# A two-block trunk on one core: wider operations in the state space setup and scan, another order of v's tiles, five tiles of u ahead

## The chip, the cores and the metric

The kernel runs on one core of a Trainium2 chip. The metric is the time of one execution on the device in microseconds (us). A core has five instruction queues that run in order, each its own: PE (matmul), DVE (vector), ACT (activation), POOL (a second, slower vector engine, which also issues gathers) and SP (which issues DMAs). PE's weight loads are listed as PEld. They meet only at semaphores. The activations, weights and tables lie in DRAM and are brought in by DMA.

## The reference

512 tokens of width 1024 pass two blocks, each a mixer and then an expert feed-forward ("peer"). Everything is float32. The second block's mixer has the state space layer that the change touches, and both blocks have the same feed-forward:

```
# state space (s5): 32 groups of 64 complex states, 16 channels each
x[t] = abar * x[t-1] + bbar @ u[t]          # abar, bbar from a, b and dt
y[t] = Re(C @ x[t]) + d * u[t]

# feed-forward (peer): 16384 experts, 8 heads, top 16 of each
scores -> top 16 pairs of keys per head -> eidx, gate
act = gelu(u[eidx] . h)                     # dot products with rows of u
out = sum(gate * act * v[eidx])             # rows of v
```

The output is the normalised sum of the residual stream after both blocks.

## The kernel before, in words

The program is written out in full, in Python, for all five queues; there is no scheduler. What sets the order is one object, `Env` (L29). Each gemm calls `E.tick()` after every 12 matmuls (L191 to 197). A tick runs functions that were deferred for it (`E.defer(n, fn)`), one step of each chain in `E.chains`, and `E.rate` steps of a filler, `E.fill`, a generator that issues a few instructions for any queue at each `yield`. `weave` (L79) makes one filler of several, each with a rate of its own. So work beside the gemms is spread over them by tick counts, and what a filler has left at the end is issued at once by `E.drain()` (L73).

Every float32 product is three matmuls, with both sides split in a high and a low part (`split`, L108: the high part by ACT at L111, the low one by DVE or POOL at L114; `mm3`, L117).

The stages, in time: the first mixer to about 625 us; the first feed-forward to 1946, whose steady stage with v begins near 1105; the second mixer to 2285; the second feed-forward, its steady stage from about 2768 to 3612.

*The setup of the state space layer* (`s5_setup`, L531) depends on weights alone. It is a filler beside the end of the first mixer: its gate gemm, `ret_out`, the merge gate and the last product (`add_gated`), then `E.flush()` and `E.drain()` at L1000 and 1001. It shares the filler with `mods`, which streams a second set of modulation weights (tile `ada`). POOL computes powers of the transition (the prelude); then come four quarters of eight groups. A quarter transposes its C on PE (L671), forms BB (L677 to 679), Q (nine powers, L688 to 690) and R (eight, L696 to 698) on POOL, multiplies Q by BB on PE (L708) and transposes R on PE (L722).

*The scan* (`Mix2.scan`, L1494) runs over 64 chunk states X on DVE, one column after the other, as a chain of the second mixer: three columns a tick. Beside it the gated recurrence of the same mixer (`scale`, `level`, `chain`, L1632 to 1700) goes between PE (ch, L1657), POOL (L1645, L1648) and DVE (tqd, L1643; tP, L1649).

*The feed-forward's steady stage* (`Peer.steady`) goes over the 128 blocks of 128 experts. The first L0 = 60 blocks had their product with u in the stage before, and their activations were put away (tile `old`); the other 68 ("new") are multiplied with u here: `s_step` loads a tile of u three ahead, splits the next and issues 24 matmuls (tile p) and a gelu (tile act). Each block then needs a tile of v: `v_load` (tile vr), `v_prep` (splits v to vh and vl, multiplies the activation by the gate G, splits that to wh and wl) and `v_mm` (18 matmuls, tile pv). The numbers at the head of `Peer` set how the two go together: LEAD tiles of u before the first v, S_END the step by which all of u is done. The fourth group of 128 tokens is done without matmuls, by POOL's gathers of rows of u and v (tile gr) and DVE's dot products and sums (L2296, L2301); SPARSE_END and VF set by which step of v these are through.

Of the kernel before, what the change touches and what calls it, by code (L numbers as in the profile page):

```python
# [526 lines left out]
TS = 8  # L527
# [3 lines left out]
def s5_setup(E, A, pool, ps):  # L531
# [133 lines left out]
    for q in range(4):  # L665
# [9 lines left out]
        tb_ = t("q1", [128, N, H], bufs=2)  # L675
# [7 lines left out]

        Q = t("Q", [128, N, TS + 1, H])
        R = t("R", [128, N, TS, H])
        for n in range(TS + 1):
            q1 = t("q1", [128, N, H], bufs=2)
            g_.tensor_tensor(Q[:, :, n, :], CT[:, 0], bc(f[:, n, 0, :]), op=ALU.mult)  # L688
            g_.tensor_tensor(q1, CT[:, 1], bc(f[:, n, 1, :]), op=ALU.mult)
            g_.tensor_tensor(Q[:, :, n, :], Q[:, :, n, :], q1, op=ALU.add)  # L690
            if n % 4 == 3:
                yield
        for n in range(TS):
            r1 = t("q1", [128, N, H], bufs=2)
            Rj = R[:, :, n, :]
            g_.tensor_tensor(Rj, BB[:, 0], bc(pw[:, n, 0, :]), op=ALU.mult)  # L696
            g_.tensor_tensor(r1, BB[:, 1], bc(f[:, n, 2, :]), op=ALU.mult)
            g_.tensor_tensor(Rj, Rj, r1, op=ALU.add)
            if n % 4 == 3:
                yield  # L700
        yield
        E.rate = E.S5_RATE
        nc.sync.dma_start(E.s5M[2, :, gs].rearrange("p g (n h) -> p g n h", h=H), Q[:, :, 1:, :])

        for g4 in range(0, N, 4):
# [92 lines left out]
class Mix1:  # L798
# [6 lines left out]
    def run(self):  # L805
# [98 lines left out]
        with tc.tile_pool(name="m1v", bufs=1) as vp:  # L904
            with tc.tile_pool(name="m1p", bufs=1, side="right") as pp:
                self.phi = pp.tile([128, 4, 512], F32R, name="phi")
                self.plo = pp.tile([128, 4, 512], F32R, name="plo")
                with tc.tile_pool(name="m1pt", bufs=1, side="right") as pt_:
                    self.pooling(pt_, pms)
                    self.keys(vp, chi, clo)  # L910
                with tc.tile_pool(name="m1f", bufs=1) as fp:
                    E.fill, E.rate = mod_filler(E, A, fp, psum, [("", m) for m in (2, 3, 4, 5)], 2, 2), 2.2
                    self.context_keys(m1, fp)
                    self.values(chi, clo)
                    for c in range(4):
                        W = ws.get()
                        for j in range(2):
                            pm = ps.tile([128, 512], F32, name="mm")
                            gemm_T(E, pm, W, self.phi, self.plo, j)
                            nc.scalar.activation(poolT[:, 2 * c + j, :], pm, AF.Copy)  # L920
                            E.tick()
                    while E.fill is not None:
                        E.tick()
                    E.flush()
                    self.context()
            with tc.tile_pool(name="m1k", bufs=1, side="right") as kp:
                self.decays(kp)
                E.flush()
# [21 lines left out]
        gp = tc.alloc_tile_pool(name="m1g", bufs=1)  # L950
        sp = tc.alloc_tile_pool(name="m1s", bufs=1)
        mods = mod_filler(E, A, Halves(E), psum, [("_2", m) for m in range(4)], 3, 2)
        E.fill, E.rate = weave((s5_setup(E, A, sp, ps), 0.6), (mods, 2.3)), 1.0
        ws.lo = ("dve",)
        rhi = gp.tile([128, 8, 512], F32R, name="rhi")
        rlo = gp.tile([128, 8, 512], F32R, name="rlo")
# [375 lines left out]
class Mix2:  # L1332
# [93 lines left out]
    def states(self):  # L1426
# [3 lines left out]
        self.X = X = self.xp.tile([128, NC5 + 1, 2, 32], F32, name="s5X")  # L1430
        Uc = up.tile([64, 32, TS, 16], F32, name="s5Uc")
        nc.gpsimd.memset(X[:, 0], 0.0)
        P1s = []
        for g8 in range(4):
            P1 = up.tile([128, 8, 128], F32, name="s5P", bufs=2)
# [50 lines left out]
    def unit_nat(self, c):  # L1486
        W = self.ws.get()
        for tb in range(4):
# [2 lines left out]
            self.nc.scalar.activation(self.vi[:, tb, 256 * c:256 * (c + 1)], pm, AF.Copy)  # L1491
            self.E.tick()

    def scan(self):  # L1494
        E, v, X = self.E, self.v, self.X
        a = self.gp.tile([128, 2, 32], F32, name="s5ra")
        b = self.gp.tile([128, 2, 32], F32, name="s5rb")
        for c in range(1, NC5):
            v.tensor_tensor(a, X[:, c], E.s5AR, op=ALU.mult)
            for i in range(2):  # L1500
                v.tensor_tensor(b[:, i, :], X[:, c, 1 - i, :], E.s5AI[:, i, :], op=ALU.mult)
            v.tensor_tensor(a, a, X[:, c + 1], op=ALU.add)
            v.tensor_tensor(X[:, c + 1], a, b, op=ALU.add)
            if c % 3 == 0:
                yield


    def s5_chunks(self):
# [217 lines left out]
class Peer:  # L1726
# [5 lines left out]
    LAG = 4  # L1732
    NQ, NT = 42, 8
    L0 = 60
    LEAD = 2
    S_END = 112
    RATE, RATE_T = 1.3, 1.3
    QT = 2
    WLO = "dve"
    SPARSE_END = 122  # L1740
    VF = 0.5

    def __init__(self, E, pfx, wq, key_rows, u, uT, v, AB, done, fill):
        self.E, self.pfx = E, pfx
# [494 lines left out]
    def v_prep(self, e, vp, spare=False):  # L2239
# [190 lines left out]
```

## Time and profile before

| | |
|---|---|
| runs | 3637.18, 3644.05, 3645.54 us; median 3644.05 |
| profiled execution | 3638.08 us, span 3636.3, granted clock 0.973 |
| PE busy | 3406.6 us, 94% of the span |
| DVE, ACT, POOL busy | 2829.1, 1380.6, 1117.7 us (78, 38, 31%) |
| moved from and to HBM | 744.52 MB read, 82.33 MB written |

Busy time is the time in which an engine has an instruction under way, and idle time is told with what ended it (the releaser). PE's share is an average: in the steady stages it is close to full, in the mixers it is not. The granted clock is PE's, 1 being 2.4 GHz. A single row's duration, on an engine that can be held up in the middle of an instruction, contains that delay.

### The profile page before, as it was taken

The page shows a single profiled execution, that of the slowest core. Times are in us where ns is not written, and L with a number is a line of the kernel's source. Part 1 is how long each engine was busy: PE and PEld are TensorE (multiplying, and loading weights), DVE is VectorE, ACT ScalarE, POOL GpSimd, SP SyncE. Part 2 cuts the span into 40 slices and gives each one's busy share as a digit, 9 for nine tenths or more (in the row PEclk, how much of TensorE's full clock was granted, in tenths as well). Part 3 has the DMA queues.
Part 4 walks back from the last instruction along what each step waited for, and adds up shares of the span by engine and source line. Part 5 has one row for each costly group of instructions (what it writes and reads, how often), then busy time and mean ns, then how long its engine had stood idle before and what let it go on. Part 6 is the DMA issues. An engine that isn't in the chain of part 4 may idle for free. (4 is left out here: it accounts for less than half of the span.)

```text
span 3636.3 us, 50853 instructions
## 1 busy us (share of the span) xinstructions
PE 3406.6 (94%) x18339; PEld 2992.4 (82%) x18339; DVE 2829.1 (78%) x6079; ACT 1380.6 (38%) x1930; POOL 1117.7 (31%) x1076
## 2 busy tenths in 40 slices
PE   8989887999998999999998888999998999999998
PEld 5878676999887888888886778899887888888886
DVE  6654743898996888888877685788996888888886
ACT  4223333332673333333334324432574333333333
POOL 3212675000003444444431432000001445444451
PEclk9999998999999999999998989999999999999999
DMA  5442754443459999999993213244457999999995
GB/s 189 137 148 71 217 172 104 131 135 126 176 201 327 359 345 352 339 338 348 329 322 115 70 57 103 95 141 139 143 206 269 341 373 325 350 341 336 348 323 193
DMA packets 418747, 830.20 MB, mean 228 GB/s; under 512 B 37948, under 2 KB 249776, under 8 KB 415424
## 3 DMA queue, kind: packets, MB, share of 16 engines
q1 hardware_dynamic: 344320, 558.41, 45.3%
q0 software_dynamic: 74176, 268.55, 20.3%
q8 instruction: 144, 2.36, 0.3%
q14 instruction: 107, 0.88, 0.1%
HBM read 744.52 MB, written 82.33 MB: 227 GB/s over the span
## 5 line engine op out<-in xcount | busy, mean ns | idle before, releaser
L2280 POOL DMA_INDIRECT gr<-in_peer_u_dram,rb x256 | 367.9, 1437 | 1406.5 <-DMA ur<-in_peer_u_tiles_dram 491.1
L118 PE MATMUL pv<-vh,wh 128*128 128x512 f32 x1512 | 602.3, 398 | 48.6 <-ACT wh L111 48.1
L120 PE MATMUL pv<-vh,wl 128*128 128x512 f32 x1512 | 604.3, 400 | 0.0
L119 PE MATMUL pv<-vl,wh 128*128 128x512 f32 x1512 | 594.6, 393 | 0.0
L2280 POOL DMA_INDIRECT gr<-in_peer_v_dram,rb x256 | 371.6, 1452 | 405.3 <-DVE accs L2301 343.0
L114 DVE TENSOR_TENSOR ul<-ur,uh 128x1024 fp32r<-128x1024 f32 x260 | 318.0, 1223 | 128.2 <-ACT uh L111 126.5
L118 PEld LDWEIGHTS pv<-vh,wh 128*128 128x128 f32 x1512 | 286.5, 189 | 126.7 <-ACT wh L111 75.2
L114 DVE TENSOR_TENSOR vl<-vr,vh 128x1024 fp32r<-128x1024 f32 x252 | 308.1, 1223 | 79.2 <-ACT vh L111 77.3
L118 PE MATMUL p<-hi,uh 128*128 128x384 f32 x1088 | 365.6, 336 | 1.4 <-ACT act L2074 1.4
L120 PE MATMUL p<-hi,ul 128*128 128x384 f32 x1088 | 365.7, 336 | 0.3 <-DVE ul L114 0.3
L119 PE MATMUL p<-lo,uh 128*128 128x384 f32 x1088 | 365.3, 336 | 0.0
L120 PEld LDWEIGHTS pv<-vh,wl 128*128 128x128 f32 x1512 | 286.1, 189 | 86.8 <-DVE wl L114 29.3
L118 PE MATMUL mm<-hi,uh 128*128 128x384 f32 x960 | 333.9, 348 | 3.6 <-ACT qT L1832 3.6
L119 PEld LDWEIGHTS pv<-vl,wh 128*128 128x128 f32 x1512 | 286.9, 190 | 52.6
L2301 DVE SCALAR_TENSOR_TENSOR accs<-gr,rb,accs 128x1024 f32<-128x1024 f32 x254 | 325.7, 1282 | 5.5 <-DMA gr<-in_peer_v_dram,rb 0.7
L120 PE MATMUL mm<-hi,ul 128*128 128x384 f32 x960 | 324.2, 338 | 4.5 <-DVE ul L114 4.5
L119 PE MATMUL mm<-lo,uh 128*128 128x384 f32 x960 | 323.0, 337 | 0.0
L2296 DVE SCALAR_TENSOR_TENSOR gr<-gr,hs 128x1024 f32<-128x1024 f32 x256 | 303.2, 1219 | 0.0
L111 ACT ACTIVATE vh<-vr 128x1024 fp32r<-128x1024 f32 x252 | 265.9, 1055 | 60.1 <-PE pv L120 30.8
L111 ACT ACTIVATE uh<-ur 128x1024 fp32r<-128x1024 f32 x260 | 272.6, 1048 | 5.5 <-DMA ur<-in_peer_u_tiles_dram 5.5
L118 PE MATMUL mm<-hi,whi 128*128 128x512 f32 (+1 forms) x656 | 262.3, 400 | 1.1 <-ACT hi L311 1.1
L120 PE MATMUL mm<-hi,wlo 128*128 128x512 f32 (+1 forms) x656 | 252.7, 385 | 1.3 <-DVE wlo L114 1.3
(625 smaller groups left out, 7079.5 us busy)
## 6 DMA issues: line engine op xcount, KB each, us to landing
ur<-in_peer_u_tiles_dram SPq DMA_DIRECT2D x256, 512.0 KB
vr<-in_peer_v_dram SPq DMA_DIRECT2D x252, 512.0 KB
raw<-in_w_in_dram SPq DMA_DIRECT2D x60, 512.0 KB
ada<-in_ada_w_dram SPq DMA_DIRECT2D x96, 256.0 KB
fG<-gst SPq DMA_DIRECT2D x12, 2048.0 KB
f_2G<-gst SPq DMA_DIRECT2D x12, 2048.0 KB
x<-in_ada_w_dram SPq DMA_DIRECT2D x64, 256.0 KB
raw<-in_peer_wq_dram SPq DMA_DIRECT2D x32, 512.0 KB
```

The source lines that it names most:

```text
L111: nc.scalar.activation(hi, src, AF.Copy)
L114: (nc.vector if e_lo == "dve" else nc.gpsimd).tensor_tensor(lo, src, hi.bitcast(F32), op=ALU.subtract)
L118: nc.tensor.matmul(out, a_hi, b_hi, start=start, stop=False)
L119: nc.tensor.matmul(out, a_hi, b_lo, start=False, stop=False)
L120: nc.tensor.matmul(out, a_lo, b_hi, start=False, stop=stop)
L2280: nc.gpsimd.indirect_dma_start(out=r, out_offset=None, in_=self.u if n < 128 else self.v, in_offset=bass.IndirectOffsetOnAxis(ap=self.eidx ...
L2296: nc.vector.scalar_tensor_tensor(r, r, 1.0, self.hs, op0=ALU.mult, op1=ALU.mult, accum_out=dots[:, j:j + 1])
L2301: nc.vector.scalar_tensor_tensor(accs, r, w[:, j:j + 1], accs, op0=ALU.mult, op1=ALU.add)
```

## The change

Five edits. (1) In the setup, Q is made in two parts of five and four powers, three POOL operations each, and R in two parts of four, three operations each on DVE; the setup's own rate in the weave goes from 0.6 to 1.0 a tick, and the line that raised the rate after a first quarter is gone. (2) The first mixer's earlier stream of modulation weights gets lag 3 for 2 and rate 2.3 for 2.2. (3) The scan goes over eight blocks of eight columns at once: seven steps inside the blocks, then seven from block to block with powers 1 to 8 of the transition, which the new `powers` computes. (4) In `Peer`, LEAD is 5 instead of 2 (the rule that orders the blocks keeps the 2, as WAIT), SPARSE_END 118 instead of 122 and VF 0.6 instead of 0.5. (5) `v_prep` issues the product with the gate first, and both of ACT's splits ahead of DVE's two.

```diff
@@ s5_setup
-        for n in range(TS + 1):
-            q1 = t("q1", [128, N, H], bufs=2)
-            g_.tensor_tensor(Q[:, :, n, :], CT[:, 0], bc(f[:, n, 0, :]), op=ALU.mult)
-            g_.tensor_tensor(q1, CT[:, 1], bc(f[:, n, 1, :]), op=ALU.mult)
-            g_.tensor_tensor(Q[:, :, n, :], Q[:, :, n, :], q1, op=ALU.add)
-            if n % 4 == 3:
-                yield
-        for n in range(TS):
...
-        yield
-        E.rate = E.S5_RATE
+        def combine(e, o, X, c0, c1, part):
+            k = part.stop - part.start
+            sh = [128, N, k, H]
+            x = [X[:, i, :, None, :].to_broadcast(sh) for i in range(2)]
+            c = [z[:, part, gs].rearrange("p n g -> p g n")[:, :, :, None].to_broadcast(sh) for z in (c0, c1)]
+            z = t("q2", [128, N, 5, H])[:, :, :k, :]
+            e.tensor_tensor(o[:, :, part, :], x[0], c[0], op=ALU.mult)
+            e.tensor_tensor(z, x[1], c[1], op=ALU.mult)
+            e.tensor_tensor(o[:, :, part, :], o[:, :, part, :], z, op=ALU.add)
+
+        for part in (slice(0, 5), slice(5, TS + 1)):
+            combine(g_, Q, CT, f[:, :, 0, :], f[:, :, 1, :], part)
+            yield
+        for part in (slice(0, 4), slice(4, TS)):
+            combine(v, R, BB, pw[:, :, 0, :], f[:, :, 2, :], part)
+            yield
+        yield
@@ Mix1.run
-                    E.fill, E.rate = mod_filler(E, A, fp, psum, [("", m) for m in (2, 3, 4, 5)], 2, 2), 2.2
+                    E.fill, E.rate = mod_filler(E, A, fp, psum, [("", m) for m in (2, 3, 4, 5)], 2, 3), 2.3
...
-        E.fill, E.rate = weave((s5_setup(E, A, sp, ps), 0.6), (mods, 2.3)), 1.0
+        E.fill, E.rate = weave((s5_setup(E, A, sp, ps), 1.0), (mods, 2.3)), 1.0
@@ Mix2
+        E.defer(2, self.powers)
...
     def scan(self):
-        for c in range(1, NC5):
-            v.tensor_tensor(a, X[:, c], E.s5AR, op=ALU.mult)
             for i in range(2):
-                v.tensor_tensor(b[:, i, :], X[:, c, 1 - i, :], E.s5AI[:, i, :], op=ALU.mult)
-            v.tensor_tensor(a, a, X[:, c + 1], op=ALU.add)
-            v.tensor_tensor(X[:, c + 1], a, b, op=ALU.add)
-            if c % 3 == 0:
-                yield
+        def add(to, frm, cR, cI):
+            v.tensor_tensor(a, frm.to_broadcast(sh), cR[:, :, None, :].to_broadcast(sh), op=ALU.mult)
             for i in range(2):
+                v.tensor_tensor(b[:, :, i], frm[:, :, 1 - i].to_broadcast(half), cI.to_broadcast(half), op=ALU.mult)
+            v.tensor_tensor(a, a, to, op=ALU.add)
+            for i in range(2):
+                v.tensor_tensor(to[:, :, i], a[:, :, i], b[:, :, i], op=ALU.subtract if i else ALU.add)
+
+        for j in range(1, 8):
+            add(Xb[:, :, j], Xb[:, :, j - 1], self.pR[:, 0:1], self.pI[:, 0:1])
+            yield
+        for k in range(1, 8):
+            add(Xb[:, k], Xb[:, k - 1, 7:8], self.pR, self.pI)
+            yield
@@ Peer
-    LEAD = 2
+    LEAD = 5
+    WAIT = 2
-    SPARSE_END = 122
-    VF = 0.5
+    SPARSE_END = 118
+    VF = 0.6
...
-            have = self.s_by[i - 1 - self.LEAD] if i > self.LEAD else 0
+            have = self.s_by[i - 1 - self.WAIT] if i > self.WAIT else 0
@@ Peer.v_prep
-        split(nc, raw, vh, vl, "act", "dve")
         act = self.act_tiles.pop(self.order[e])
         a3 = act.rearrange("p (c t) -> p c t", t=self.TB)
         nc.vector.tensor_tensor(a3, a3, G, op=ALU.mult)
-        split(nc, act, wh, wl)
+        nc.scalar.activation(vh, raw, AF.Copy)
+        nc.scalar.activation(wh, act, AF.Copy)
+        nc.vector.tensor_tensor(vl, raw, vh.bitcast(F32), op=ALU.subtract)
+        nc.vector.tensor_tensor(wl, act, wh.bitcast(F32), op=ALU.subtract)
```

On PE, the end of the first mixer, before: the last product (mm, whi and rhi), one small transpose, and then all that is left of the setup, until L1902 begins the feed-forward. s5Q, s5BB and s5R are the setup's tiles.

```order
2560 L120 MATMUL mm<-whi,rlo 128x256
2561 L272 MATMUL p_5385<-ident,ss 128x128
2562 L708 MATMUL p_5394<-s5Q,s5BB 16x128 x4
2563 L708 MATMUL p_5404<-s5Q,s5BB 16x128 x4
2564 L722 MATMUL p_5415<-ident,s5R 128x128 x4
2565 L722 MATMUL p_5421<-ident,s5R 128x128 x4
2566 L671 MATMUL p_5428<-ident,s5cn 128x128 x2
2567 L708 MATMUL p_5512<-s5Q,s5BB 16x128 x4
2568 L708 MATMUL p_5522<-s5Q,s5BB 16x128 x4
2569 L722 MATMUL p_5533<-ident,s5R 128x128 x4
2570 L722 MATMUL p_5539<-ident,s5R 128x128 x4
2571 L1902 MATMUL ch<-ident,hi_4746 128x128 x8
```

And of the changed kernel (L1935 is the line that was L1902):

```order
2568 L119 MATMUL mm<-wlo,rhi 128x256
2569 L120 MATMUL mm<-whi,rlo 128x256
2570 L272 MATMUL p_5330<-ident,ss 128x128
2571 L1935 MATMUL ch<-ident,hi_4763 128x128 x8
2572 L1935 MATMUL ch<-ident,hi_4766 128x128 x4
```

Nine rows of the setup have left this place. The first product of Q with BB stands at row 1936 before and at row 1789 now (L710), and the last transpose of R at 2570 before and 2352 now (L724).

On ACT, where the first steady stage begins (uh: the high part of a tile of u; act: the gelu of its product p), before:

```order
487 L111 ACTIVATE uh<-ur 128x1024
488 L2074 ACTIVATE act<-p_10478 128x384
489 L111 ACTIVATE uh<-ur 128x1024
490 L2074 ACTIVATE act<-p_10519 128x384
491 L111 ACTIVATE vh<-vr 128x1024
492 L111 ACTIVATE wh<-old 128x384
493 L111 ACTIVATE vh<-vr 128x1024
494 L111 ACTIVATE wh<-old 128x384
```

Now:

```order
491 L2107 ACTIVATE act<-p_10311 128x384
492 L111 ACTIVATE uh<-ur 128x1024
493 L2107 ACTIVATE act<-p_10344 128x384
494 L111 ACTIVATE uh<-ur 128x1024
495 L2107 ACTIVATE act<-p_10377 128x384
496 L111 ACTIVATE uh<-ur 128x1024
497 L2107 ACTIVATE act<-p_10410 128x384
498 L2288 ACTIVATE vh<-vr 128x1024
499 L2289 ACTIVATE wh<-old 128x384
500 L2288 ACTIVATE vh<-vr 128x1024
```

Three more activations of u stand ahead of the first vh. On DVE at the same place (old: an activation put away, Go: its gates), before:

```order
1025 L114 TENSOR_TENSOR ul<-ur,uh 128x1024 x4
1026 L114 TENSOR_TENSOR vl<-vr,vh 128x1024
1027 L2255 TENSOR_TENSOR old<-old,Go 128x384
1028 L114 TENSOR_TENSOR wl<-old,wh 128x384
1029 L2296 SCALAR_TENSOR_TENSOR gr,rb<-gr,hs 128x1024
```

Now:

```order
1050 L114 TENSOR_TENSOR ul<-ur,uh 128x1024 x7
1051 L2287 TENSOR_TENSOR old<-old,Go 128x384
1052 L2290 TENSOR_TENSOR vl<-vr,vh 128x1024
1053 L2291 TENSOR_TENSOR wl<-old,wh 128x384
1054 L2331 SCALAR_TENSOR_TENSOR gr,rb<-gr,hs 128x1024
```

The product with the gate has moved ahead of vl, so that wh, which needs it, no longer stands behind vl.

## Rows read from the trace of the kernel before

**Rows 1.** Busy time by stage: stretch, length, PE, PEld, DVE, ACT, POOL, clock, DMA.

```profile
380.00:460.00 80.00, 68.76 (x283) 53.30 (x282) 55.36 (x84) 28.20 (x38) 67.73 (x138) 0.94 0.71 224
590.00:627.00 37.00, 12.53 (x57) 9.64 (x57) 1.20 (x3) 7.36 (x17) 22.38 (x57) 0.58 0.38 76
2045.00:2172.00 127.00, 102.46 (x579) 89.52 (x578) 115.69 (x405) 28.85 (x39) 49.51 (x51) 0.88 0.14 42
3000.00:3400.00 400.00, 398.15 (x1927) 345.10 (x1926) 334.88 (x413) 141.25 (x191) 192.25 (x133) 1.00 0.95 340
```

**Rows 2.** PE's waits: us, times, longest; from 580 us first, then 380 to 590.

```profile
PE p L708 <- POOL s5Q L690: 10.7, 1, 10.7
...
PE p L708 <- POOL s5Q L690: 8.5, 1, 8.5
```

**Rows 3.** Timeline of DVE behind the seam: start, us, line; idle before in brackets.

```profile
624.70 0.88 DVE L305 SCALAR_TENSOR_TENSOR nz<-p,AB,rb 128x256 f32<-128x256 f32 x2 [35.05 <-PE p L295]
```

**Rows 4.** Timeline of POOL: first operation of the prelude, and last of BB.

```profile
385.70 0.38 POOL L574 TENSOR_TENSOR s5wr<-s5a,s5dt 128x32 f32<-128x32 f32 x1 [27.70 <-ACT s5dt L571]
...
455.32 0.46 POOL L679 TENSOR_TENSOR s5BB<-s5BB,s5q 128x128 f32<-128x128 f32 x1
```

**Rows 5.** Groups on POOL, 597 to 620 us: busy us, mean ns, idle before.

```profile
L690 POOL TENSOR_TENSOR s5Q<-s5Q,s5q 128x128 f32<-128x128 f32 x9 | 4.1, 453 | 0.7
```

**Rows 6.** Groups on DVE, 2045 to 2172 us: the scan, and a 512-column operation.

```profile
L1503 DVE TENSOR_TENSOR s5X<-s5ra,s5rb 128x64 f32<-128x64 f32 x63 | 23.2, 368 | 2.1
L1501 DVE TENSOR_TENSOR s5rb<-s5X,s5AI 128x32 f32<-128x32 f32 x126 | 22.6, 220 | 0.0
L1499 DVE TENSOR_TENSOR s5ra<-s5X,s5AR 128x64 f32<-128x64 f32 x63 | 22.0, 350 | 1.6
L1502 DVE TENSOR_TENSOR s5ra<-s5ra,s5X 128x64 f32<-128x64 f32 x63 | 16.4, 261 | 0.0
...
L1637 DVE TENSOR_TENSOR tqd<-tq,tP 128x512 f32<-128x512 f32 x2 | 1.4, 682 | 0.0
```

**Rows 7.** POOL and DVE in the scan: two timeline rows, then two of POOL's groups.

```profile
2060.82 2.41 POOL L114 TENSOR_TENSOR wlo<-raw,whi 128x1024 fp32r<-128x1024 f32 x1 [2.23 <-ACT whi L111]
...
2061.03 2.28 DVE L1503 TENSOR_TENSOR s5X<-s5ra,s5rb 128x64 f32<-128x64 f32 x1
...
L1648 POOL TENSOR_TENSOR tS<-tS,tP 128x256 f32<-128x256 f32 x21 | 17.1, 813 | 1.3
L1645 POOL TENSOR_TENSOR tkd<-tk,tS 128x256 f32<-128x256 f32 x17 | 13.9, 815 | 36.5 <-PE ch L1657 16.3 <-DVE tr L1706 8.2 <-DVE s5ra L1499 6.3
```

**Rows 8.** PE's longest wait, 2045 to 2172 us.

```profile
PE ch L1657 <- DVE tqd L1643: 15.4, 9, 3.9
```

**Rows 9.** Timeline of PE and ACT at the first tile of v.

```profile
1128.10 0.80 PE L118 MATMUL pv<-vh,wh 128*128 128x512 f32 x1 [9.85 <-ACT wh L111]
...
1124.71 1.06 ACT L111 ACTIVATE vh<-vr 128x1024 fp32r<-128x1024 f32 x1 [5.93 <-DMA vr<-in_peer_v_dram]
...
2794.57 0.79 PE L118 MATMUL pv<-vh,wh 128*128 128x512 f32 x1 [12.71 <-ACT wh L111]
```

**Rows 10.** Timeline of PE in a tile of u, three matmuls apart.

```profile
1135.01 0.34 PE L118 MATMUL p<-hi,uh 128*128 128x384 f32 x1
...
1135.54 0.34 PE L118 MATMUL p<-hi,uh 128*128 128x384 f32 x1
```

**Rows 11.** Timeline of a late tile of v: ACT, then DVE.

```profile
3592.60 0.52 ACT L111 ACTIVATE wh<-old 128x384 fp32r<-128x384 f32 x1 [1.82 <-DVE old L2255]
...
3590.82 1.23 DVE L114 TENSOR_TENSOR vl<-vr,vh 128x1024 fp32r<-128x1024 f32 x1 [3.85 <-ACT vh L111]
3591.96 0.55 DVE L2255 TENSOR_TENSOR old<-old,Go 128x384 f32<-128x384 f32 x1
```

**Rows 12.** PE's waits for v's splits: 1110 to 1946 us, then 2780 to 3620.

```profile
PE pv L118 <- ACT wh L111: 20.2, 11, 9.8
...
PE pv L118 <- ACT wh L111: 25.8, 12, 12.7
```

More of the change, by code (lines that the diff above doesn't have):

```diff
@@ L674, in s5_setup @@
         BB = t("BB", [128, 2, N, H])
-        tb_ = t("q1", [128, N, H], bufs=2)
+        tb_ = t("q1", [128, N, H])
         for i, w in ((0, cim), (1, cis)):
@@ L685, in s5_setup @@
         R = t("R", [128, N, TS, H])
-        for n in range(TS + 1):
-            q1 = t("q1", [128, N, H], bufs=2)
-            g_.tensor_tensor(Q[:, :, n, :], CT[:, 0], bc(f[:, n, 0, :]), op=ALU.mult)
-            g_.tensor_tensor(q1, CT[:, 1], bc(f[:, n, 1, :]), op=ALU.mult)
-            g_.tensor_tensor(Q[:, :, n, :], Q[:, :, n, :], q1, op=ALU.add)
-            if n % 4 == 3:
-                yield
-        for n in range(TS):
[L694 to L699, printed above, removed]
-                yield
+        def combine(e, o, X, c0, c1, part):
[13 more added lines that the diff above has]
+            yield
         yield
-        E.rate = E.S5_RATE
         nc.sync.dma_start(E.s5M[2, :, gs].rearrange("p g (n h) -> p g n h", h=H), Q[:, :, 1:, :])
@@ L1492, in unit_nat, with powers @@
             self.E.tick()
-    def scan(self):
-        E, v, X = self.E, self.v, self.X
-        a = self.gp.tile([128, 2, 32], F32, name="s5ra")
-        b = self.gp.tile([128, 2, 32], F32, name="s5rb")
-        for c in range(1, NC5):
-            v.tensor_tensor(a, X[:, c], E.s5AR, op=ALU.mult)
-            for i in range(2):
-                v.tensor_tensor(b[:, i, :], X[:, c, 1 - i, :], E.s5AI[:, i, :], op=ALU.mult)
-            v.tensor_tensor(a, a, X[:, c + 1], op=ALU.add)
-            v.tensor_tensor(X[:, c + 1], a, b, op=ALU.add)
-            if c % 3 == 0:
-                yield
+    def powers(self):
+        E, v, gp = self.E, self.v, self.gp
+        self.pR, self.pI = pR, pI = [gp.tile([128, 8, 32], F32, name=n) for n in ("s5pR", "s5pI")]
+        a, b = (self.gate[i][:, :256].rearrange("p (j g) -> p j g", g=32) for i in (2, 3))
+        v.tensor_copy(pR[:, 0], E.s5AR[:, 0])
+        v.tensor_copy(pI[:, 0], E.s5AI[:, 0])
+        n = 1
+        while n < 8:
+            lo, hi, sh = slice(0, n), slice(n, 2 * n), [128, n, 32]
+            cR, cI = (p[:, n - 1:n].to_broadcast(sh) for p in (pR, pI))
+            v.tensor_tensor(a[:, lo], pR[:, lo], cR, op=ALU.mult)
+            v.tensor_tensor(b[:, lo], pI[:, lo], cI, op=ALU.mult)
+            v.tensor_tensor(pR[:, hi], a[:, lo], b[:, lo], op=ALU.subtract)
+            v.tensor_tensor(a[:, lo], pR[:, lo], cI, op=ALU.mult)
+            v.tensor_tensor(b[:, lo], pI[:, lo], cR, op=ALU.mult)
+            v.tensor_tensor(pI[:, hi], a[:, lo], b[:, lo], op=ALU.add)
+            n *= 2
@@ new lines, in scan @@
+    def scan(self):
+        v, X = self.v, self.X
+        a, b = (self.gate[i].rearrange("p (j i g) -> p j i g", i=2, g=32) for i in (2, 3))
+        Xb = X[:, 1:].rearrange("p (b j) i g -> p b j i g", j=8)
+        sh, half = [128, 8, 2, 32], [128, 8, 32]
+        def add(to, frm, cR, cI):
+            v.tensor_tensor(a, frm.to_broadcast(sh), cR[:, :, None, :].to_broadcast(sh), op=ALU.mult)
+            for i in range(2):
+                v.tensor_tensor(b[:, :, i], frm[:, :, 1 - i].to_broadcast(half), cI.to_broadcast(half), op=ALU.mult)
[8 more added lines that the diff above has]
+            yield
```

## The prediction, made before the run

> **What bounds the kernel.** I read first the busy time by stage. In a steady stage of the expert feed-forwards PE is busy 398.15 of 400 us while the DMA engines stand at 0.95 [rows 1]: PE sets the time there and DMA is just behind it. PE has room only at seams, so I read next what ended its idle time at the seams that the change touches. There are four. At the end of the first mixer, 590 to 627 us, PE works 12.53 of 37 us at a granted clock of 0.58 (mostly the lower level, 1.2 GHz). In the state space scan, 2045 to 2172 us, DVE works 115.69 of 127 us and PE 102.46, at 0.88 [rows 1]. The other two are the first tile of v in each feed-forward, and the short waits of PE for v's splits behind it.
>
> **Setup (A).** In the seam at 590 us one wait of PE for POOL's Q is 10.7 us [rows 2], and DVE sits idle for 35.05 us before the next stage [rows 3]: POOL is doing the last quarters of the setup in 128-column operations. A quarter has 27 of these for Q and 24 for R, 453 ns each for the third of a triple with DVE silent [rows 5], at most 51 x 0.45 = 23 us. After the change it has six Q operations of 640 and 512 columns on POOL and six R operations of 512 on DVE. DVE's price is in the trace, 682 ns for 512 columns [rows 6], so 4.1 us a quarter. POOL's price for 512 to 640 columns is not; it lies between the 0.45 us of 128 columns and the 2.41 of 1024 [rows 5, 7]. I take 1.4, between the two by the columns: Q then takes 8 us for some 12, and R leaves POOL. More important is the step rate, 1.0 instead of 0.6 a tick: by the order the setup's last transpose stands at PE's row 2352 instead of 2570, inside the gemms, with nothing left for the seam. There, the 37 us less 12.53 of PE's work are 24.5, and much of that work runs at the lower clock and is cheaper among gemms. I take 33 us off the seam and 4 onto the gemms.
>
> Against it stands the start. POOL's prelude runs from 385.70, when the step size is there, to the end of BB at 455.8 [rows 4], 70 us, and PE already waits 8.5 us for the first Q [rows 2]. Now the first product with Q stands 147 rows earlier (1789 for 1936). With 283 matmuls in the 80 us of that stretch [rows 1], 147 are 42 us. Some of it comes back, as the prelude is issued three ticks of 12 matmuls earlier, 10 us, and the rest is a stall unless POOL gets faster. DVE is worse placed than PE: R needs BB and now stands in DVE's queue ahead of the splits of weights, so while DVE waits, PE runs out of weights. The stall lies between the old 8.5 and 8.5 + 42 - 10 = 40 us; I take 26, near the middle, since POOL's prelude then runs beside less of DVE's work, and 3 for loads that the setup's own now stand in front of. Less the old 8.5 this is 20. A is -33 + 4 + 20 = -9; I take -8, with bounds of -25 (no stall) and +15 (40 us, and the seam's gain 4 smaller).
>
> **The earlier stream of ada (B).** Rate and lag change in a stretch before 380 us that the rows don't show; the edit moves steps by less than a load of 256 KB. I take -1 (bounds -5 and +1).
>
> **Scan (C).** Before, 63 columns of five operations are busy for 23.2 + 22.6 + 22.0 + 16.4 = 84.2 us [rows 6] of DVE's 115.69. After, there are 14 steps of two 512-column and four 256-column operations. 512 cost 682 ns; 256 lie between the 220 of 32 columns and that [rows 6], and I take 430. A step is 2 x 0.68 + 4 x 0.43 = 3.1 us, 14 are 43, and the 20 small operations of the powers, at some 0.25, are 5 more, put ahead of the scan. DVE is relieved by some 36 to 40 us where PE waits 15.4 us in nine waits for DVE's tqd [rows 8], which stands behind scan columns in DVE's queue. PE cannot gain more than its idle time, 127 - 102.46 = 24.5 us, and a little by the clock; and the loop from PE over POOL's 256-column operations back to DVE stays. I take half, -13, with bounds of -22 and +4.
>
> What speaks against wide operations is in the trace too: a scan operation that takes 0.22 us elsewhere starts at 2061.03 and lasts 2.28, to the end of POOL's 1024-column operation begun at 2060.82 [rows 7]. One of the two waits the other out. Where POOL is the one that waits, a wide operation of DVE costs it up to 0.68 us instead of 0.22. POOL has 21 + 17 operations of 256 columns here [rows 7], in the loop that PE waits for: 38 x 0.46 = 17 us at the most, and C would be -13 + 17 = +4. That is the third rival. The Trainium skill has this as a rule (SBUF — State Buffer, section "SBUF: two separate sides"): a VectorE operation with two SBUF inputs and a GpSimd one that reads SBUF take a shared port pair as an exclusive lock for the whole instruction. The trace agrees, with its 2.28 us; by the rule the sum would be 17 us worse, and I weigh it low since the longest of POOL's waits needs the worst meeting each time.
>
> **Five tiles of u ahead (D1).** The first product with v waits 9.85 us in the first feed-forward and 12.71 in the second; ACT's split of that tile had waited 5.93 for it to come from memory [rows 9]. Now three more tiles of u stand ahead on PE, each 24 matmuls, three in 0.53 us [rows 10]: 4.2 us each, 12.5 in all. They are no new work but come out of the steady stage, where PE is full, so a gap filled is a gain. The new limit is ACT's queue, where vh now stands behind the activation of the fifth tile of u: PE waits at least for that (384 columns as wh, 0.52), vh 1.06 and wh 0.52, 2.1 us, and with vl some 2.6. The gain is 9.85 - 2.6 + 12.71 - 2.6 = 17. Three more loads of 512 KB now compete with v's first ones, and with DMA at 0.95 the steady stage may take part of it back: -14, bounds -22 and 0.
>
> **Order of v's splits and the sparse end (D2).** In a tile's chain now stand vh on ACT, vl 1.23 on DVE, the product with the gate 0.55 and wh 0.52, for which ACT waits 1.82 on DVE [rows 11]: 1.06 + 1.23 + 0.55 + 0.52 = 3.4 us from the start of vh to the first matmul. After it, the product goes first, wh stands straight behind vh (1.6), and vl, at 1.06 + 1.23, is wanted one matmul of 0.4 later (1.9): up to 1.5 us less at a wait. There are ten waits of 20.2 - 9.8 us in all behind the first, and eleven of 25.8 - 12.7 [rows 12], 1.1 us on the mean. If none were left, 23 us would go. But a wait that begins with a late tile keeps that part, and the sparse rows, done four tiles sooner, put their accumulation and a third buffer of v among the last splits. I take -10, bounds -22 and +6.
>
> **Sum.** -8 - 1 - 13 - 14 - 10 = -46 from the profiled execution's 3638.08 us (span 3636.3): 3592. The three timed runs have their median at 3644.05, 6 us above it; I add 4 of these: 3596.
>
> **Rivals.** (1) *POOL's prelude eats the seam's gain.* The wait of 8.5 us that is there already speaks for it; that nothing of the setup is left for the seam in any case speaks against. A is +8 instead of -8: 3612. (2) *DMA becomes the bound of the steady stage.* Its 0.95 speaks for it; that PE is short of only 1.85 in 400 us speaks against. D1 and half of D2 come back, 19 us: 3615. (3) *POOL waits out the wide scan operations*: 3596 + 17 = 3613. (4) *Slower: R blocks DVE in every quarter.* It decides where POOL's 12 operations of a quarter take longer than the 11 ticks ahead of R, 11 x 12 matmuls or 37 us; then the stall of 26 us comes in three more quarters: 3596 + 78 = 3674; with two, 3648. By the rows 6 x 0.46 + 6 x 1.4 = 11 us, and 29 with every one at 2.41, so it needs a dearer POOL than any row shows. (5) *The seams' waits only move*, since data arrive no earlier: A +6, B 0, C -2, D1 -4 and D2 -2, with the 4 of the median 3640.
>
> **Chances.** Forecast 0.55; (1) 0.12; (2) 0.10; (3) 0.08; (4) 0.07; (5) 0.08. The range is 3566 to 3637: below, three fifths of the 50 us by which the lower bounds undercut the terms (17, 4, 9, 8 and 12); above, the edge of (5). It leaves about 0.1 on each side. A measurement of this kernel cannot tell less than 0.2%, 7 us, from no change, so faster means below 3637: the forecast and (1) to (3), 0.85. Within: 0.08, mostly (5). Slower: 0.07, (4).
>
> **What would show it.** A: no wait of PE for Q or R in the seam, DVE's idle time there a few us, and instead a long wait of DVE for POOL's BB in the first quarter. C: DVE under 90 us busy over the scan, the waits for tqd halved. D1: a first wait for v of 2 to 3 us at both places. D2: ACT's wh no longer waits for DVE's product, and PE's waits for wh are below 1 us in the mean. I am wrong if the time is above 3637: then DVE waits for BB in several quarters, or the steady stages show new waits on loads of u and v.

## The result, and the profile after

| | before | changed |
|---|---|---|
| median (runs) | 3641.76 us (3637.18 to 3645.54) | 3598.45 us (3597.34 to 3602.52) |
| ratio, 95% interval | 1 | 0.9883 (0.9871 to 0.9896) |
| profiled execution, span | 3636.3 us | 3595.6 us |

One execution of this study, of the scan alone, took 4197.64 us at a granted clock of 0.745 where the others have 0.97 to 0.98, and no ratio counts it.

The forecast was 3596 us. The sum is right to 2.5 us, but the terms are not, as the stages of the two profiled executions show. Each boundary is the start of a matmul that both programs have, read from the timeline; the last pv before stand at 1962.2 and 3627.6 us.

| stretch of PE | before | changed | difference | forecast |
|---|---|---|---|---|
| start to the first gemm of the first feed-forward | 626.7 | 634.8 | +8.1 | -9 (A, B) |
| from there to the first p beside v | 482.2 | 485.3 | +3.0 | 0 |
| first p to last pv, first feed-forward | 853.3 | 835.3 | -17.9 | -12 (half of D1, D2) |
| last pv to the first p of the second | 809.6 | 799.6 | -9.9 | -13 (C) |
| first p to last pv, second feed-forward | 855.9 | 831.9 | -24.0 | -12 (half of D1, D2) |

The rows of the changed kernel that answer to [rows 1] come first: stretch, length, PE, PEld, DVE, ACT, POOL, clock, DMA share and GB/s. The seam lies earlier or later with its work, so the second stretch is 590 to 640 us here, and the scan's 2035 to 2152.

```profile
380.00:460.00 80.00, 49.79 (x196) 38.67 (x195) 43.14 (x69) 21.25 (x31) 59.13 (x136) 0.78 0.45 138
590.00:640.00 50.00, 48.17 (x373) 46.41 (x373) 25.45 (x55) 22.02 (x44) 0.00 (x0) 0.93 0.36 101
2035.00:2152.00 117.00, 99.35 (x577) 87.93 (x576) 103.53 (x176) 28.07 (x38) 55.77 (x53) 0.88 0.16 46
3000.00:3400.00 400.00, 400.00 (x1962) 355.96 (x1961) 342.99 (x419) 140.16 (x196) 186.85 (x140) 1.00 0.99 357
```

The seam is gone (PE 48.17 of 50 us), and the hole now stands at 380 to 460 us, where PE works 49.79 us for 68.76 before. Look at the last row's counts: PE was busy 398.15 of 400 us before and is 400.00 now, which is 0.5%, but it has 1962 matmuls there instead of 1927, 1.8% more. Busy time did not show what was lost.

PE's longest wait from 380 to 640 us answers to [rows 2]. It ends at 450.30 us, with POOL's Q. DVE has two waits for POOL in the same time, ended at 440.95 and 450.27 us.

```profile
PE p L710 <- POOL s5Q L696: 21.1, 1, 21.1
```

```profile
DVE s5R L694 <- POOL s5BB L679: 14.9, 1, 14.9
...
DVE s5q L695 <- POOL s5Q L696: 8.5, 1, 8.5
```

PE's wait is for Q itself, asked for before POOL has it, and not for DVE. The first of DVE's is R asking for BB before POOL has it. The second isn't needed by the data: R's scratch on DVE is the same tile, in one buffer, as Q's on POOL (`t("q2", ...)` in `combine`), so R has to wait until POOL is done with Q.

In the scan, DVE's groups from 2035 to 2155 us (busy us, mean ns), and POOL's two in the loop of PE, answer to [rows 6, 7]:

```profile
L1527 DVE TENSOR_TENSOR gate<-s5X,s5pI 128x256 f32<-128x256 f32 x28 | 20.3, 764 | 0.0
L1530 DVE TENSOR_TENSOR s5X<-gate,gate 128x256 f32<-128x256 f32 x28 | 14.5, 559 | 0.5
L1528 DVE TENSOR_TENSOR gate<-gate,s5X 128x512 f32<-128x512 f32 x14 | 12.7, 905 | 0.0
...
L1525 DVE TENSOR_TENSOR gate<-s5X,s5pR 128x512 f32<-128x512 f32 x14 | 11.7, 832 | 0.1
```

```profile
L1680 POOL TENSOR_TENSOR tS<-tS,tP 128x256 f32<-128x256 f32 x21 | 19.3, 920 | 1.3
L1677 POOL TENSOR_TENSOR tkd<-tk,tS 128x256 f32<-128x256 f32 x17 | 15.5, 909 | 27.7 <-PE ch L1689 21.0 <-DVE tr L228 6.6
```

Scan operations take 59.2 us of DVE instead of 84.2, not the 43 of the forecast: a 256-column one takes 559 to 764 ns in the mean and not 430. The two lines' means hide two kinds. The 35 of these 56 operations that none of POOL's overlaps took 0.41 to 0.43 us; the other 21 took 0.42 to 2.58, 1.06 in the mean. Of the 512-column ones, 15 without POOL took 0.68 to 0.69 us and 13 beside it 1.08 in the mean. Two pairs in the timeline, the first beside a 1024-column operation of POOL, the second without one:

```profile
2052.27 2.83 POOL L114 TENSOR_TENSOR wlo<-raw,whi 128x1024 fp32r<-128x1024 f32 x1 [1.78 <-ACT whi L111]
2052.81 2.91 DVE L1527 TENSOR_TENSOR gate<-s5X,s5pI 128x256 f32<-128x256 f32 x2
...
2065.21 0.75 DVE L1527 TENSOR_TENSOR gate<-s5X,s5pI 128x256 f32<-128x256 f32 x2
```

So the forecast's prices are those of an operation alone, and the rest is the meeting with POOL. POOL's 38 operations have become 0.10 us longer each. PE's waits for tqd have gone from 15.4 us in nine [rows 8] to this, over 2035 to 2152 us:

```profile
PE ch L1689 <- DVE tqd L1675: 8.8, 5, 4.5
```

At the first tile of v (timeline of PE, then of ACT; [rows 9]) the wait has moved on to the fourth tile of u, whose load came late:

```profile
1143.29 0.69 PE L118 MATMUL p<-hi,uh 128*128 128x384 f32 x1 [3.87 <-ACT act L2107]
1152.31 0.50 PE L118 MATMUL pv<-vh,wh 128*128 128x512 f32 x1 [1.94 <-ACT wh L2289]
...
1141.80 1.06 ACT L111 ACTIVATE uh<-ur 128x1024 fp32r<-128x1024 f32 x1 [6.87 <-DMA ur<-in_peer_u_tiles_dram]
```

And of PE's waits for v's splits there are three in each feed-forward (1085 to 1960 us, then 2740 to 3592), most of their time in one long one each. Before, there were twelve in each: [rows 12] stops at 1946 us, and to the last pv its first line is 22.4 us in twelve, not 20.2 in eleven (first line here, 1110 to 1970 us; then the changed kernel's two).

```profile
PE pv L118 <- ACT wh L111: 22.4, 12, 9.8
...
PE pv L118 <- ACT wh L2289: 14.3, 3, 12.1
...
PE pv L118 <- ACT wh L2289: 9.3, 3, 7.2
```

The long one is new. In the timeline of ACT and DVE around 1919 us, wh waits for the product with the gate, and that stands in DVE's queue behind an operation of the fourth token group that waits for a row of gates (gr) from memory:

```profile
1919.33 0.52 ACT L2289 ACTIVATE wh<-old 128x384 fp32r<-128x384 f32 x1 [11.32 <-DVE old L2287]
...
1916.64 0.69 DVE L2362 TENSOR_TENSOR vr<-accs,gr 128x512 f32<-128x512 f32 x1 [14.11 <-DMA gr<-gate]
```

Before, the same operation at 1938.87 us waited for nothing of the kind. The load of that row was issued at 1907.56 us now, when DVE stood waiting already, and at 1927.46 us before, 11 us ahead of its use.

Of the signs that the prediction named, those of A came (no wait for Q or R at the seam, a long one of DVE for BB), and so did that of D1: a first wait of 1.94 us, and of 1.9 in the second feed-forward. That of C came in part: the waits for tqd went from 15.4 to 8.8 us, but DVE is busy for 103.53 us over the scan and not under 90. That of D2 did not: wh still waits for the product, for 11.32 us at 1919 us.

### The profile page after: what moved, and what is told of

It is laid out like the page before. It is cut to its first block, busy times and chain, and to the rows that moved or that the text cites. A ratio compares the mean times of both kernels' runs of the same rounds, so it can differ in the third digit from the quotient of the medians.

```text
span 3595.6 us, 50475 instructions
## 1 busy us (share of the span) xinstructions
PE 3391.0 (94%) x18339; PEld 3016.6 (84%) x18339; DVE 2818.0 (78%) x5892; ACT 1358.1 (38%) x1930; POOL 979.2 (27%) x896
## 4 chain that ended last, share of the span: by engine, by line
PE 73%; DVE 16%; DMA 4%; issue 2%; ACT 2%; POOL 2%; SPq 1%; DVEq 0%; ACTq 0%; POOLq 0%
PE pv L119 9%; PE pv L118 9%; PE pv L120 9%; PE mm L118 8%; PE mm L119 8%; PE mm L120 8%; DVE ga L2068 5%; PE p L118 5%; PE p L120 5%; PE p L119 5%; DVE gb L2064 3%; DMA ada<-in_ada_w_dram 2%; DVE ul L114 1%; DMA x<-in_ada_w_dram 1%; PE ch L1945 1%
## 5 line engine op out<-in xcount | busy, mean ns | idle before, releaser
L2315 POOL DMA_INDIRECT gr<-in_peer_u_dram,rb x256 | 337.2, 1317 | 1472.9 <-DMA ur<-in_peer_u_tiles_dram 1032.6
L118 PE MATMUL pv<-vh,wh 128*128 128x512 f32 x1512 | 591.7, 391 | 23.6 <-ACT wh L2289 23.6
L120 PE MATMUL pv<-vh,wl 128*128 128x512 f32 x1512 | 590.7, 391 | 0.0
L2315 POOL DMA_INDIRECT gr<-in_peer_v_dram,rb x256 | 343.6, 1342 | 390.8 <-DVE accs L2336 332.8
L2107 ACT ACTIVATE act<-p 128x384 f32<-128x384 f32 x136 | 66.9, 492 | 702.1 <-PE p L120 681.1
```

The source lines that it names most:

```text
L118: nc.tensor.matmul(out, a_hi, b_hi, start=start, stop=False)
L120: nc.tensor.matmul(out, a_lo, b_hi, start=False, stop=stop)
L2315: nc.gpsimd.indirect_dma_start(out=r, out_offset=None, in_=self.u if n < 128 else self.v, in_offset=bass.IndirectOffsetOnAxis(ap=self.eidx ...
```

## The experiments

Each part was put alone on the kernel before. Then the changed kernel was run with a pause added and with one part taken back, and last came versions drawn from these.

### The order of v's splits alone

```diff
-        split(nc, raw, vh, vl, "act", "dve")
...
         nc.vector.tensor_tensor(a3, a3, G, op=ALU.mult)
-        split(nc, act, wh, wl)
+        nc.scalar.activation(vh, raw, AF.Copy)
+        nc.scalar.activation(wh, act, AF.Copy)
+        nc.vector.tensor_tensor(vl, raw, vh.bitcast(F32), op=ALU.subtract)
+        nc.vector.tensor_tensor(wl, act, wh.bitcast(F32), op=ALU.subtract)
```

> The kernel before with one edit: v_prep's new order (gate product first, both of ACT's splits ahead of DVE's two). Theory W: the old order held back the weight loads of nearly every tile of v by a fraction of a microsecond, which shows as idle time of PEld and not of PE; in the trace of before the gap between two pv matmuls of 400 us in the steady stage is 0.235 us in the mean, after 0.227, and 2268 such gaps give 18 us a feed-forward. With the visible late waits of 8 us gone too, it expects 22 to 26 us a feed-forward, in all 3592 to 3600 us. Rival P, the recorded term D2: only the waits that PE shows are at stake, 10 us in all, 3630. Rival E: the pace of the steady stage came from the five tiles ahead, then this alone gives under 5 us a feed-forward.

Measured: 3590.52 us against 3643.91, ratio 0.986 (0.9843 to 0.9877). That is 53 us, more than the whole change brings. From the first pv to the last, the first feed-forward goes from 834.1 to 808.9 us and the second from 833.0 to 804.5. Theory W is right, a little small. PE's visible waits for the splits, 48.2 us in both stretches before, fall to these (1110 to 1940 us, then 2755 to 3577), the first tile's being nearly all that is left:

```profile
PE pv L118 <- ACT wh L2256: 13.0, 5, 11.1
...
PE pv L118 <- ACT wh L2256: 11.4, 2, 10.9
```

That is 24 of the 53 us. The rest is pace. This is PEld's view of waits in the kernel before, 3000 to 3400 us (us, times, longest), which the prediction had not read:

```profile
PEld pv L118 <- ACT wh L111: 7.2, 22, 1.2
PEld pv L120 <- DVE wl L114: 7.1, 24, 0.3
```

Weight loads of pv waited in 22 and 24 places for 14.3 us in 400, a third of a microsecond each, over the 59 tiles of v there, old and new. In this kernel the same view of the same stretch has no wait, and PE gets through 1967 matmuls instead of 1927, 2% more; over the two stretches of 853 and 856 us that makes some 35 us by estimate, for the 29 that are left:

```profile
3000.00:3400.00 400.00, 400.00 (x1967) 356.59 (x1967) 337.28 (x409) 139.78 (x197) 181.73 (x137) 1.00 0.98 350
```

### Five tiles of u alone

```diff
-    LEAD = 2
+    LEAD = 5
+    WAIT = 2
...
-            have = self.s_by[i - 1 - self.LEAD] if i > self.LEAD else 0
+            have = self.s_by[i - 1 - self.WAIT] if i > self.WAIT else 0
```

> The kernel before with one edit: LEAD 5, with the order of the blocks held by WAIT 2. Theory T: the seam is carried by the loads, so the wait for v only moves to the tiles of u; from the first p to the first pv the trace of before has 19.2 and 22.8 us for two tiles, after 32.3 and 32.1 for five, and three tiles are worth 12.5. It expects a gain of 0 to 1 us in the first feed-forward, 2 to 4 in the second, 3637 to 3641 in all. Rival P, the recorded term D1: 14 us, 3628. Rival E: the five tiles also keep the later stage fed, then 30 us or more.

Measured: 3643.12 us against 3643.91, ratio 0.9999 (0.9988 to 1.001): nothing that shows, nearest to theory T, which had 3 to 7 us less. PE's waits from 1110 to 1160 us, where before has 9.85 and 0.58:

```profile
PE p L118 <- ACT act L2075: 5.6, 4, 3.9
PE pv L118 <- ACT wh L111: 3.8, 1, 3.8
```

The sum is nearly the same. T's reason, that the loads carry this seam whatever is put first, holds for the place, but not for the worth of the edit: see the versions below.

### The earlier end of the sparse rows alone

```diff
-    SPARSE_END = 122
-    VF = 0.5
+    SPARSE_END = 118
+    VF = 0.6
```

> The kernel before with one edit: SPARSE_END 118 and VF 0.6. Theory G: ending the sparse rows earlier puts DVE's update of the fourth token group, which waits for a load of the gate row that is issued late, ahead of tiles of v still to be prepared; the changed kernel has single waits of 12.1 and 7.2 us there, where before has four of 8.0 and 7.7 in all. It expects 3 to 10 us more than before, 3645 to 3652. Rival P: it is a part of the gain of the last tiles, 2 to 6 us less than before.

Measured: 3667.70 us against 3643.91, ratio 1.0068 (1.0049 to 1.0087): 24 us slower. Theory G has the sign and the place, and is too small by more than half. PE's waits for v's splits, 1110 to 1985 and 2800 to 3660 us, for 22.4 and 25.8 before, and the DVE operation behind the longest of the first line (in the second the longest is the first tile's, and the end has one of 11.9):

```profile
PE pv L118 <- ACT wh L111: 38.4, 14, 13.3
...
PE pv L118 <- ACT wh L111: 37.8, 13, 13.4
```

```profile
1930.99 0.69 DVE L2327 TENSOR_TENSOR vr<-accs,gr 128x512 f32<-128x512 f32 x1 [13.02 <-DMA gr<-gate]
```

### The wide setup alone

```diff
-        for n in range(TS + 1):
...
+        for part in (slice(0, 5), slice(5, TS + 1)):
+            combine(g_, Q, CT, f[:, :, 0, :], f[:, :, 1, :], part)
+            yield
+        for part in (slice(0, 4), slice(4, TS)):
+            combine(v, R, BB, pw[:, :, 0, :], f[:, :, 2, :], part)
+            yield
...
-        E.fill, E.rate = weave((s5_setup(E, A, sp, ps), 0.6), (mods, 2.3)), 1.0
+        E.fill, E.rate = weave((s5_setup(E, A, sp, ps), 1.0), (mods, 2.3)), 1.0
```

> The kernel before with one edit: the setup's wide Q and R with R on DVE, and its rate 1.0. Theory S: the seam at 590 us gives back 35 us and the first quarter takes the same away again, in a wait of PE for Q of about 21 us that stands behind DVE's wait of 15 us for BB, and 12 to 15 us in smaller ones. It expects the first gemm of the feed-forward within 4 us of before, 3638 to 3646 in all. Rival P, the recorded term A: 8 us less, 3634. Rival B: what the changed kernel lost by 212 us was the setup's doing too; not so if this kernel is even with before up to 360 us.

Measured: 3647.48 us against 3643.91, ratio 1.0008 (0.9997 to 1.0018), and the first gemm of the feed-forward 4.1 us later. Theory S. The two waits are the changed kernel's, PE's first and then DVE's:

```profile
PE p L710 <- POOL s5Q L696: 19.9, 1, 19.9
```

```profile
DVE s5R L694 <- POOL s5BB L679: 14.9, 1, 14.9
```

Up to 353 us this kernel is 2.2 us behind before. Seven other kernels that are like before up to there stand between 2.4 us ahead of it and 5.5 behind, so nothing shows that what the changed kernel lost until then (6.4 us) is the setup's doing: nothing speaks for rival B. The 4.1 us can be chance too, since a kernel with the first mixer of before comes to the feed-forward's first gemm up to 5.3 us later than before does.

### The earlier ada stream alone

```diff
-                    E.fill, E.rate = mod_filler(E, A, fp, psum, [("", m) for m in (2, 3, 4, 5)], 2, 2), 2.2
+                    E.fill, E.rate = mod_filler(E, A, fp, psum, [("", m) for m in (2, 3, 4, 5)], 2, 3), 2.3
```

> The kernel before with one edit: the earlier ada stream's lag 3 and rate 2.3. Profiles of kernels without the edit stand 0 to 5.6 us behind before at 246 us (mean 1.9), those with it 4.6 to 6.4. Theory D: the edit asks for tiles no sooner than the loads bring them and puts one more wait at 210 us, so it costs 3 to 5 us: 5 to 6 us behind before at 246 us. Rival P, the recorded term B: nothing to tell, 0 to 2 us behind.

Measured: 3644.39 us against 3643.73, ratio 1.0002 (0.9992 to 1.0011), and 2.8 us behind before at 246 us in the profile, between the two theories. That stretch varies by up to 8 us between kernels that are the same in it. Whether the edit costs a few us stays open; nothing shows that it brings any.

### The scan alone

```diff
+        E.defer(2, self.powers)
...
-        for c in range(1, NC5):
...
+        for j in range(1, 8):
+            add(Xb[:, :, j], Xb[:, :, j - 1], self.pR[:, 0:1], self.pI[:, 0:1])
+            yield
+        for k in range(1, 8):
+            add(Xb[:, k], Xb[:, k - 1, 7:8], self.pR, self.pI)
+            yield
```

> The kernel before with one edit: the scan in eight blocks. Theory L: DVE and POOL hold each other up, so the wide operations save DVE some 25 us (84 to 59 in the changed kernel's rows) and not 40, and the second mixer is shorter by 9 to 11 us, 3632 to 3636 in all. Rival P, the recorded term C: 13 us or more, 3630 or less. Rival X, the recorded third rival: POOL's waits eat it, no gain.

Measured: ratio 0.9984 (0.9971 to 0.9997), median 3638.37 us against 3641.96; in the profile the stretch from the last pv to the first p of the second feed-forward goes from 809.6 to 799.9 us. The stretch agrees with theory L; the times, at 6 us by the ratio, give 1 to 11. (In this profile the two feed-forward stretches, which the edit does not touch, came out 5.4 and 3.2 us longer.) Neither rival fits the stretch, and the other profiles bear it out: it is 806.2 to 812.3 us in the six kernels without the new scan and 798.4 to 803.4 in the seven with it. The wait for tqd, over 2045 to 2165 us, is as in the changed kernel:

```profile
PE ch L1687 <- DVE tqd L1673: 8.4, 4, 4.5
```

### The changed kernel with a pause in the setup

```diff
+    for _ in range(8):
+        yield
     for q in range(4):
         gs = slice(q * N, (q + 1) * N)
```

> The changed kernel with eight empty steps of the setup between the prelude and the first quarter, so that R and Q come to DVE and PE some eight ticks later, while the setup still ends inside the gemms. Theory S: PE's wait of 21 us and DVE's of 15 + 8 us come from asking for BB before POOL has it; they shrink to under 5 us and the seam stays empty: 18 to 26 us less than the changed kernel, 3573 to 3581. Rival Q: POOL's prelude is slowed as much by the extra DVE work that now runs beside it, and the wait only moves: 3590 to 3600. Rival R: the later setup comes out at the seam again, the same 3590 to 3600, but with waits after 580 us.

Measured: 3576.02 us against the changed kernel's 3598.45, 22 us less (ratio to before 0.9817, 0.9797 to 0.9838). The stretch to the feed-forward's first gemm is 15.1 us shorter in the profiles, and the rest lies within what executions differ by. Theory S, in the main: DVE's wait for BB is gone, but what is left of PE's for Q isn't under the 5 us expected, and DVE's own for Q, by the shared scratch, has stayed (360 to 640 us):

```profile
PE p L712 <- POOL s5Q L698: 7.2, 1, 7.2
```

```profile
DVE s5q L697 <- POOL s5Q L698: 8.5, 1, 8.5
```

POOL did not get faster: from its first operation to the end of BB it takes 69.5 us here and 58.1 in the changed kernel, where DVE stood still for 14.9 of them. That is what rival Q had in mind, but PE's first product with Q now stands behind gemm work that it stood ahead of, and it comes only 9.7 us later. So the stall came from the asking.

### The changed kernel with the sparse end as before

```diff
-    SPARSE_END = 118
-    VF = 0.6
+    SPARSE_END = 122
+    VF = 0.5
```

> The changed kernel with SPARSE_END 122 and VF 0.5 as before. Theory G: the earlier end of the sparse rows costs; alone on the kernel before it cost 24 us, of it 12 in one wait at each end of v's stage, which the changed kernel has too, at 12.1 and 7.2 us. It expects those two waits gone and 12 to 24 us less than the changed kernel, 3574 to 3586. Rival H: with the new order of splits the earlier end does no harm beyond those two waits and helps against the accumulation at the end, so that under 8 us come back, 3591 to 3598.

Measured: 3574.83 us, 24 us less than the changed kernel (ratio to before 0.982, 0.98 to 0.984), the top of theory G. PE's waits for v's splits, 1110 to 1945 and 2745 to 3570 us:

```profile
PE pv L118 <- ACT wh L2289: 3.7, 4, 1.9
...
PE pv L118 <- ACT wh L2289: 1.9, 1, 1.9
```

The visible waits explain 18 of the 24 us (14.3 + 9.3 - 3.7 - 1.9); where the other 6 were is open.

### Versions drawn from the runs

The changed kernel with the pause, and with LEAD, the sparse end and the ada stream as before:

> A version drawn from the runs: the changed kernel's splits, scan and wide setup, with the eight empty steps before the first quarter, and with LEAD 2, SPARSE_END 122, VF 0.5 and the earlier ada stream's lag and rate as before. If the parts add: 3590.5 of the splits alone, less 10 for the scan, less 20 for the setup without its stall, 3560. If the seams and the DMA bound make them overlap: 3570 to 3580. It should beat both the kernel before and the changed one in either case.

Measured: 3567.26 us, ratio to before 0.9796 (0.9779 to 0.9813). Faster than the last two, and 7 us short of the full sum. Next, the same with one number changed:

```diff
-    LEAD = 2
+    LEAD = 5
```

> The version s10_best with one edit, LEAD 5 instead of 2. In the profile of s10_best the stretch from the first p to the last pv is 829.3 and 825.2 us long, with waits of 11 us for the first v; in s8_sparse122, which has LEAD 5 and the same splits and sparse end, 825.0 and 820.7. Theory V: once the splits no longer hold PE back, five tiles ahead do what they were put in for, and give 8 to 9 us: 3557 to 3560. Rival T: LEAD stays worth nothing, as it was alone, 3565 to 3569.

Measured: 3556.43 us, ratio 0.9763 (0.9748 to 0.9779), 11 us less by the medians and 7 by the means, with two of the five executions among those of the last version. In the profiles the stretches from the first p to the last pv are 4.6 and 3.4 us shorter, and from the last version to the changed kernel with the sparse end as before, which has LEAD 5 too, they are 4.3 and 4.5 shorter. Theory V: an edit that was worth nothing on the kernel before is worth some 8 us here. That it is the order of the splits that makes the difference, and not the new setup or scan, no run shows: LEAD 5 was not run with the splits alone. PE's waits with LEAD 2 (1090 to 1925 us), then with LEAD 5:

```profile
PE pv L118 <- ACT wh L2291: 13.4, 5, 11.3
```

```profile
PE p L118 <- ACT act L2109: 4.1, 4, 2.4
PE pv L118 <- ACT wh L2291: 3.5, 4, 1.9
```

One step more, on the same kernel:

```diff
-        E.fill, E.rate = weave((s5_setup(E, A, sp, ps), 1.0), (mods, 2.3)), 1.0
+        E.fill, E.rate = weave((mods, 2.3), (s5_setup(E, A, sp, ps), 1.0)), 1.0
```

> The version s11_lead5 with one edit: the two fillers change places in the weave, so that the first three loads of the second ada stream go out ahead of the setup's own twelve. In the changed kernel the loads the other way round made DVE wait 10.1 us for the first tile and put PE some 8 us back by 378 us. Theory O: the order of the first loads does it; that wait falls to below 5 us and the kernel is 4 to 8 us faster than s11_lead5. Rival N: the setup's prelude starts as much later, and the wait for POOL's Q takes it all: within 3 us.

Measured: 3552.93 us (3549.33 to 3555.88), ratio 0.9746 (0.9732 to 0.9761), 3.5 us less than the last, between the two theories, and not clear of noise, since the two intervals overlap. The wait in question did fall as theory O says, from 10.2 us to 4.5 (DVE, 360 to 600 us):

```profile
DVE x L498 <- DMA x<-in_ada_w_dram: 4.5, 1, 4.5
```

As rival N has it, a part moved: PE now waits 5.0 us for a load of the setup (s5an), 2.1 in the last version. By its median this is the fastest version of the study, 91 us under the kernel before and 45 under the changed one.

## Why the prediction was right in the sum, and where its terms were not

| term | forecast | alone, on the kernel before | what the runs showed |
|---|---|---|---|
| A, setup | -8 | +3 (-1 to +7) | seam and stall as forecast, more delay around them |
| B, ada stream | -1 | +1 (-3 to +4) | nothing to tell |
| C, scan | -13 | -6 (-11 to -1) | 9.6 us in its stretch |
| D1, five tiles | -14 | 0 (-4 to +4) | some -8 in a version with the new splits |
| D2, splits | -10, with the sparse end | -51 (-57 to -45) | waits of PE, and more of weight loads |
| D2, sparse end | | +25 (+18 to +32) | DVE behind a late load |

(Alone: the ratio of each run times 3642 us.) The parts alone add up to some -28 us and the whole change brings -43. D1, if it is worth its 8 us in the changed kernel too, is half of the difference; the intervals are wide enough for the rest. So the total of 3596 came out by errors that cancel: D2's two parts gave 26 us where their term has 10, and A, C and D1 gave less than theirs. That was luck.

**A.** The seam went as worked out: a matmul that ends the first mixer's gemms stands 43.4 us late and the first of the next stage 8.1, so the seam gave back 35.3, for 33 in the forecast. The stall was also named and placed rightly: the gemm's matmul at 404.5 us before is 13.2 late, the one at 419.5 is 39.4 late, 26.2 between the two, and the forecast has 26. It came by PE's own product with Q, which waited 21.1 us. The other way that the prediction gave, DVE behind BB leaving PE without operands, does not show: PE's wait right behind, for rhi, is 2.8 us, and at the same matmul before it was 3.0. What the forecast left out is 6.7 us more by 456 us of the time before, most of it in a second wait of PE, for a product of the ada stream whose tiles came late from memory:

```profile
495.39 1.87 PE L472 MATMUL p<-x,ones 128*1 128x512 f32 x2 [7.49 <-DVE x L500]
...
494.58 0.75 DVE L500 SCALAR_TENSOR_TENSOR x<-x,s 128x512 f32<-128x512 f32 x1 [4.76 <-DMA x<-in_ada_w_dram]
```

Before the stall, where the setup's loads now stand ahead of the ada ones, 6.8 us were lost and not 3. What remains is 6.7 of small delays against the 4 that it had. Less 9.4 for the old wait, A came to +2 in that execution, and the stage row's +8.1 contains 6.4 from before the setup begins.

**C.** The mechanism held and its size was off: the step "256 lie between the 220 of 32 columns and that, and I take 430". They took 559 to 764 in the mean, and 512 took 832 to 905 for 682. Alone, they took 0.42 and 0.68 us, as forecast: what the step left out is the meeting with POOL, which fell on 21 of the 56 and 13 of the 28, though [rows 7] has such a meeting. The third rival had the reverse effect in mind and priced it at up to 17 us; POOL's 38 operations grew by 0.10 us each, 4 us. The stretch shrank by 9.6 to 9.9.

**D1.** The failed step is "the new limit is ACT's queue". The queue did give the 1.94 us wait, but a load of u came 6.87 us late ahead of it: alone, the edit left 9.4 us of PE's waits at this seam for 10.4 before. DMA moved 380 GB/s from 1110 to 1140 us already before. The prediction had seen the three more loads there and priced them at 3 us; how much they took back no run shows by itself. Yet the edit isn't worthless: in the version with the new splits it gives some 8 us.

**D2.** Two edits were put into one term with opposite signs. For the splits the failed step is "there are ten waits of 20.2 - 9.8 us": these are waits that PE shows, 23 us at the most by [rows 12], and the edit alone brought 51. The edit took away nearly all of them, some 23 us, where the term had 10 for both edits; the larger part of the gain was in weight loads that waited a third of a microsecond in 46 places of 400 us, which the term put at nothing. That the chain of vh, vl, product and wh was what held the tiles up was right. For the sparse end, the prediction named the accumulation among the last splits, and not the row of gates that it waits for with DVE's queue behind it.

**The second rival** (DMA as the bound of the steady stage) did not come: DMA stands at 0.99 and 357 GB/s there now, PE at 400.00 of 400 us, and PEld has no wait from 3000 to 3400 us.

## What to carry to other kernels

Read the waits of the weight loads beside those of PE: this stage showed PE busy 398.15 of 400 us and still lost 2% in them, which the count of matmuls in equal stretches told. Before an operation goes to an engine that has other work queued behind it, ask when its operands are there and what else its scratch tile serves; eight empty steps ahead of the same work were worth 22 us by the medians, 15 of them in the stage itself. And put no two edits in one term: of the six here, one gave more than the whole, one took half of that back, and one that was worth nothing alone gave some 8 us beside the others.

## What the hardware showed that was not expected

DMA could be driven beyond what looked like its limit in the steady stage, from 0.95 and 340 GB/s to 0.99 and 357, with no new wait of PE. A 256-column operation of DVE took 0.41 to 0.43 us where none of POOL's overlapped it and 1.06 in the mean, at most 2.58, where one did, while POOL's operations grew by only 0.10 us each when DVE's became wider: DVE bore most of what the wider operations cost here.
